# Five places in the engines' instruction lists of a two-layer encoder kernel

## The chip, the cores and the metric

The kernel runs on one core of a Trainium2 chip. A core has a matrix engine (TensorE, PE in the profile; its weight loads are PEld), a vector engine (VectorE, DVE), a scalar engine (ScalarE, ACT), a general engine (GpSimd, POOL) and an engine that here issues transfers (SyncE, SP). Each works through its own list of instructions in order and waits at an instruction until what it needs is there. The metric is the device time of one execution in microseconds; the median of the runs counts.

## The reference

The input is 1024 tokens of width 1024. Layer 0 projects the normed tokens once, and feeds a diagonal state-space part with a gated linear unit (GLU) and a retention part; both are gated, joined and projected back. Layer 1 is a convolution of width 31. Cut to what the change lies in:

```python
def s5_mixer(...):                       # y of the state-space scan
    y = jax.nn.gelu(y)
    y = y * jax.nn.sigmoid(y @ glu_w + glu_b)

def retention(q, k, v):                  # 8 heads, chunks of 64 tokens
    q = rope(q, positions) * (RET_DK ** -0.5)
    k = rope(k, positions)
    ...

def mixer_ab(h, ...):
    u_s5, g_s5, q, k, v, g_ret = jnp.split(h @ w_in, cuts, axis=-1)
    y_s5 = s5_mixer(u_s5, ...) * jax.nn.silu(g_s5)
    y_ret = retention(q, k, v) * jax.nn.silu(g_ret)
    return jnp.concatenate([y_s5, y_ret], axis=-1) @ w_out

def mixer_conv(h, ...):
    a, b, g = jnp.split(h @ w_in, 3, axis=-1)
    u = depthwise_conv(a * jax.nn.sigmoid(b), conv_w) + conv_b
    u = jax.nn.silu(layernorm(u)) * jax.nn.silu(g)
    return u @ w_out
```

Each layer is x + mixer(rmsnorm(x)), and a last rmsnorm ends it. All is float32.

## The kernel before

Everything lies in tiles of 128 partitions; a product works on 128 x 512 halves of the tokens. For accuracy each operand of a matmul is split into a high part in the matmul's reduced type (made by a copy on ACT, names ending in h, wh_...) and a low part, the remainder (names ending in l, wl_...), and `mm3` (lines 217 to 226) makes each product of three: high by high (line 224), high weight by low operand (225) and low weight by high operand (226). Weights come in as wf_..., ACT makes wh_... (line 213), and POOL or DVE makes wl_... (line 214).

The program is written out in one long order by a tile framework. `tc.issue_after(i)` puts what is issued within it behind instruction i in the list of its engine; a scheduler decides the rest by priorities. Tiles with the same tag share a few buffers, so that a new one waits for the last use of an old one: the tag "tp" has three (`load_split`, 1346). At the end `order` (lines 287 to 301) adds a set of pairs (engine, late, early): in that engine's list the n-th instruction that writes the tile `late` has to stand behind the n-th that writes `early`. Such a pair adds no wait between engines; it sets the order within one list, and the scheduler places everything else around it.

The stages that matter, in the order of time:

- `retention` (1070) goes through four pairs of heads. For each it makes keys and queries (`ret_proj`, 1121: kraw, qraw on DVE at 1138; turned by a rotary product on POOL at 1151 and 1153, krot, qrot and the swapped halves kswp, qswp), values (`ret_values`, 1171, three matmuls at 1185 to 1187 and an ACT copy at 1188; for the first pair `ret_values_wide`, 1193, matmuls 1209 to 1211, with the low weights wl_v0_0_j) and the heads (`ret_heads`).
- Between them lies work of the state-space part. `y_pass(k)` (1020) loads y (yp, line 1027), takes its GELU on ACT (1031, yn), stores it (1033), makes four differences of its quarters on DVE (1039 to 1042), splits these and stores the parts (1048, 1049, t_d). `glu_sums(g)` (1051) loads quarters of the GLU's weights (gs0, gs1, line 1058), combines them on DVE (1062 to 1065) and stores the sums (1068, ws_d). These serve a product in seven block multiplications instead of eight.
- `layer0_back_and_layer1` (1336) makes the GLU. `load_split` (1346) loads an operand (line 1356), and `split` (1331) makes its high part on ACT (1332) and its low part on DVE (1334), with an optional `behind`. `product` (1386) puts four k-blocks of `mm3` into a bank. The last of the block multiplications, at 1459 to 1474, makes mm_glu5n of yt1, adds u3 into a spare bank on DVE (mm_gluz, line 1470), goes on in the same bank with y22 and adds u2 (1473). `gated` (1396) loads the gate yg and yn (1398, 1400), takes a tanh on ACT (1409), multiplies on POOL (1401) and DVE (1414) and splits the result (ysh 1416, ysl 1418).
- Then line 1475 loads the retention's results as operands (yr0 for the first half of the tokens, yr1 for the second, eight tiles each), and `w_out` multiplies both by the output weights (mm_wo, with the weights wos and wor).
- Layer 1: `h1` (1500) makes the normed operands (h1h 1513, h1l 1514), `ab` the products and u (1542), `conv` (1566) the convolution, a chain of taps on DVE (1607), for which ACT and POOL make partial sums (tp at 1575, 1579, 1580, copied to a bank at 1586). Its norm takes sums over partitions by matmuls of ones (cst, 557) and a square root and reciprocal (523, 524).

Of the kernel before, what the change touches and what calls it, by code (L numbers as in the profile page):

```python
# [15 lines left out]
ALU = mybir.AluOpType  # L16
# [6 lines left out]
KB = 8  # L23
# [13 lines left out]


LANES = 2


def s5_order():

    seq = []
    for b in range(8):
        g, h = 8 + 2 * b, 9 + 2 * b
        turns = [(f"m0_{b}", 0), (f"m1_{b}", 0)]
        kern = [(f"Kg_{b}", 0), (f"Kg_{b}", 1)]
        z = [(f"v{c}_{b}", n) for n in range(4) for c in range(2)]
        back = [(f"d0_{b}", 0), (f"d1_{b}", 0), *z[6:], (f"S_{b}", 0), (f"S_{b}", 1)]  # L50
        w = [(f"{t}_{b + 1}", n) for t, n in (("W2r", 0), ("W2i", 0), ("pw0", 0), ("pw1", 0), ("W2r", 1), ("W2i", 1))]
        w = w if b < 7 else []
        seq += [*kern, *turns, *z[:6]]
        if b:
            seq += [*back, (f"gt_{g}", 0), (f"wl_g{h}", 0), *w[:3], (f"gt_{g}", 1), *w[3:]]
        else:
            seq += [(f"gt_{g}", 0), *w, *back, (f"gt_{g}", 1)]
        seq += [(f"gt_{h}", 0), *([(f"wl_g{g + 2}", 0)] if b < 7 else []), (f"gt_{h}", 1)]
    return [("PE", ("mm_g8_0", 6), ("v1_0", 7)),
            *(("Activation", (f"pw0_{b + 1}", 0), (f"gt_{8 + 2 * b}", 0)) for b in range(1, 7)),  # L60
            *(("DVE", late, early) for early, late in zip(seq, seq[1:]))]
# [4 lines left out]
def mv(ap):  # L66

    return ap.rearrange("p (a c) -> p c a", a=LANES)


def un(ap):

    return ap.rearrange("p (c a) -> p a c", a=LANES)


def nat(ap):

    return ap.rearrange("p (a c) -> p a c", a=LANES)

# [15 lines left out]
class Trunk:  # L95
# [148 lines left out]
    def run(self):  # L244
        tc, nc, A = self.tc, self.nc, self.A
        self.ps_mm = self.pool("ps_mm", 3, PSUM)
        self.cp = self.pool("cp")
        self.wp = self.pool("wp")
        self.opA = self.pool("opA", 16)
        self.dram = self.pool("dram", 1, DRAM)  # L250

        self.ident = self.cp.tile([P, P], F32, name="ident")
        make_identity(nc, self.ident)
        self.ones = self.cp.tile([P, P], F32, name="ones")
        nc.vector.memset(self.ones[:], 1.0)
        self.ones_r = self.cp.tile([P, P], F32R, name="ones_r")
        nc.vector.tensor_copy(self.ones_r[:], self.ones[:])
        self.epst = self.cp.tile([P, 1], F32, name="epst")
        nc.vector.memset(self.epst[:], EPS)
        self.mhalf = self.cp.tile([P, KB], F32, name="mhalf")  # L260
        nc.vector.memset(self.mhalf[:], -0.5)
        self.warm = self.cp.tile([P, 1], F32, name="warm")
        nc.scalar.copy(self.warm[:], self.ones[:, 0:1])

        dt = lambda n, shape: self.dram.tile(shape, F32, name=n)
        self.u_d = dt("u_d", [8, 8, 16, 8, P])
        self.y_d = dt("y_d", [8, 8, 16, 8, P])
        self.k_d = dt("k_d", [8, 112 + P, P])
        self.gs_d = dt("gs_d", [D, T])
        self.gr_d = dt("gr_d", [D, T])  # L270
        self.yn_d = dt("yn_d", [D, T])
        self.yr_d = dt("yr_d", [D, T])
        self.t_d = dt("t_d", [2, 2, HALF, T])
        self.x1_d = dt("x1_d", [D, T])

        with ExitStack() as mid:
            self.mid = self.pool("mid", 1, stack=mid)
            with ExitStack() as st:
                self.layer0_front(st)
            with ExitStack() as st:  # L280
                self.ps_aux = self.pool("ps_aux", 5, PSUM, stack=st)
                self.retention(st)
        with ExitStack() as st:
            self.layer0_back_and_layer1(st)
        self.order(s5_order())

    def order(self, pairs):

# [15 lines left out]
    def layer0_front(self, st):  # L304
# [107 lines left out]
        def u_block(nb):  # L412
            ut = uv.tile([P, 8, P], F32, name=f"ut_{nb}", tag="ut", bufs=2)

            def evac(h, ps):
                r = self.R[:, h * HALF:(h + 1) * HALF]
                o = ut[:, ::-1, h * 64:(h + 1) * 64].rearrange("p j (a m) -> p j a m", a=LANES)

                with self.tc.issue_after(self.u_evac[0].ins) if nb == 1 else nullcontext():
                    self.u_evac[nb] = nc.vector.tensor_tensor(  # L420
                        o, ps[:].rearrange("p (m j a) -> p j a m", j=8, a=LANES),
                        r.rearrange("p (a m j) -> p j a m", j=8, a=LANES), op=ALU.mult)
            if nb < 3:
# [912 lines left out]
    def layer0_back_and_layer1(self, st):  # L1336
        nc, A = self.nc, self.A
        v, gp = nc.vector, nc.gpsimd
# [4 lines left out]
        hs = lambda h: slice(h * HALF, (h + 1) * HALF)  # L1343
        rows = lambda k: slice(k * P, (k + 1) * P)

        def load_split(parts, name, h, wide, behind=None):

            res = []
            for i, part in enumerate(parts):
                if wide:  # L1350
                    if i % 2 == 0:
                        f2 = self.wp.tile([P, 2, HALF], F32, name=f"{name}f{i}", tag="wf", bufs=3)
                    f = f2[:, i % 2, :]
                else:
                    f = lp.tile([P, HALF], F32, name=f"{name}f{i}", tag="tp", bufs=3)[:]
                nc.sync.dma_start(f, part)
                a, b = (self.op_tile(self.opA, f"A{h}", f"{name}{q}{i}") for q in "hl")
                self.split(f, a, b, v, behind)
                res.append((a, b))
            return res  # L1360
# [21 lines left out]
        u3 = [opB.tile([P, HALF], F32, name=f"gu3_{n}", tag="B1") for n in range(4)]  # L1382
# [3 lines left out]
        def product(ps, w, a, x, more=False):  # L1386

            for k in range(4):
                self.mm3(ps[:], w, 4 * a + k, (x[k][0][:], x[k][1][:]), k == 0 and not more, k == 3, more)

        def spare(name, n):
            return ps_cv.tile([P, HALF], F32, name=name, tag=("cv", "cn")[n % 2])

        held = []

        def gated(nb, h, z, turned=False):
            yg = lp.tile([P, HALF], F32, name=f"yg{nb}_{h}", tag="u", bufs=5)
# [27 lines left out]
        for m in range(2):  # L1425
            pss = [self.bank(f"mm_glu1{2 * m + a}", aux=False) for a in range(2)]
# [13 lines left out]
        for i, x in ((6, t2), (7, t3), (4, t4)):  # L1440
            for m in range(2):
# [5 lines left out]
                for a in range(2):  # L1447
                    n = 2 * m + a
                    ps = self.bank(f"mm_glu{i}{n}", aux=False)
                    product(ps, w, a, x)  # L1450
                    if i == 4:
                        z = spare(f"mm_gluy{n}", n)
# [8 lines left out]
        for m in range(2):  # L1461
            pss = [self.bank(f"mm_glu5{2 * m + a}", aux=False) for a in range(2)]
            for i, x in ((5, t1), (3, b22)):
                w = wn()
                for a in range(2):
                    n = 2 * m + a
                    product(pss[a], w, a, x, i == 3)
                    if i == 5:
                        z = spare(f"mm_gluz{n}", n)
                        v.tensor_tensor(nat(z[:]), un(u3[n][:]), un(pss[a][:]), op=ALU.add)  # L1470
                        gated(4 + n, 1, z, True)
                    else:
                        v.tensor_tensor(pss[a][:], u2[n][:], pss[a][:], op=ALU.add)
                        glu_end = gated(n, 1, pss[a])
        yr = [load_split([self.yr_d[rows(k), hs(h)] for k in range(KB)], f"yr{h}", h, False) for h in range(2)]


        hx = [None, None]
# [521 lines left out]
```

## Time and profile before

| | |
|---|---|
| median of three runs | 1142.86 us (1140.91, 1142.86, 1143.72) |
| profiled execution, its own time | 1140.13 us |
| its span, first to last instruction | 1138.3 us |
| mean granted TensorE clock | 0.997 |
| busy: PE, DVE, ACT, POOL | 1119.0, 832.9, 492.3, 640.0 us |
| HBM read and written | 182.53 MB, 74.65 MB |

A row of a group or of the timeline names the line of the code, the engine, the operation and the tiles as out<-in (numbers of the tiles left out), with its start and duration in microseconds; what is in square brackets at its end is the idle time of the engine just before it and what ended that. The rows of waits give who waited, for whom, and how long in total, how often and at most. A window gives each engine's busy time in a stretch. A matmul's duration overlaps the next one's, so what TensorE loses is read from the starts.

### The profile page before, as it was taken

What the parts mean: (1) busy time and instruction counts of PE and PEld (TensorE: products, weight loads), DVE (VectorE), ACT (ScalarE), POOL (GpSimd) and SP (SyncE); (2) the same over time, 40 slices, a digit from 0 to 9 for tenths busy, and PEclk for the clock granted to TensorE, in tenths of its full rate; (3) what the DMA queues carried; (4) which work ended last, traced back from release to release, by engine and by line L of the source; (5) the groups of instructions that cost most, each with busy time, mean ns of one, the idle gap of its engine ahead of it and who ended that gap; (6) DMA issues with size and microseconds to landing.
All of it is one profiled execution on the core that took longest, in us unless ns stands there. A gap on an engine that the chain in (4) does not pass through costs nothing.

```text
span 1138.3 us, 17193 instructions
## 1 busy us (share of the span) xinstructions
PE 1119.0 (98%) x6278; PEld 979.4 (86%) x6278; DVE 832.9 (73%) x1478; ACT 492.3 (43%) x723; POOL 640.0 (56%) x448
## 2 busy tenths in 40 slices
PE   9999999999999999999999999999999999999897
PEld 7888888888888889898888888888888888888786
DVE  7973967777417469587669523599999899999744
ACT  6422433333223231333546324455536676444673
POOL 2059999888136454332674110688534568677663
PEclk9999999999999999999999999999999999999999
DMA  9345555553487866869998987666678655367865
GB/s 356 111 132 158 195 181 180 170 176 133 150 263 251 302 221 176 314 194 348 390 354 290 339 298 268 222 218 211 221 269 293 222 188 173 111 205 243 285 225 189
DMA packets 118181, 262.51 MB, mean 231 GB/s; under 512 B 10704, under 2 KB 42320, under 8 KB 117456
## 3 DMA queue, kind: packets, MB, share of 16 engines
q1 hardware_dynamic: 114640, 248.82, 64.8%
q10 hardware_dynamic: 3456, 12.58, 2.7%
q8 instruction: 49, 0.80, 0.3%
q14 instruction: 36, 0.29, 0.1%
HBM read 182.53 MB, written 74.65 MB: 226 GB/s over the span
## 4 chain that ended last, share of the span: by engine, by line
PE 74%; DMA 10%; DVE 8%; ACT 3%; issue 2%; POOL 1%; SPq 1%; POOLq 0%; DVEq 0%; ACTq 0%
PE mm_g L224 6%; PE mm_g L225 6%; PE mm_g L226 6%; PE mm_wo L225 5%; PE mm_wo L224 5%; PE mm_wo L226 5%; DMA yp<-y_d 2%; PE mm_b L225 2%; PE mm_b L226 2%; PE mm_a L226 2%; PE mm_a L225 2%; PE mm_b L224 2%; PE mm_a L224 2%; PE mm_oc L226 2%; PE mm_oc L225 2%
## 5 line engine op out<-in xcount | busy, mean ns | idle before, releaser
L1607 DVE SCALAR_TENSOR_TENSOR cv<-u,convw,cv 128x512 f32<-128x512 f32 x398 | 273.0, 748 | 6.5 <-ACT cv L1586 4.5
L1580 POOL TENSOR_TENSOR tp<-tp,tp 128x512 f32<-128x512 f32 x64 | 83.1, 1298 | 33.8 <-ACT tp L1579 32.8
L224 PE MATMUL mm_g<-xh,wh_g 128*128 128x512 f32 x256 | 97.9, 382 | 0.0
L225 PE MATMUL mm_g<-xl,wh_g 128*128 128x512 f32 x256 | 97.0, 379 | 0.0
L226 PE MATMUL mm_g<-xh,wl_g 128*128 128x512 f32 x256 | 95.7, 379 | 0.0
L485 POOL TENSOR_TENSOR s1q<-s1q,s1q 128x512 f32<-128x512 f32 x12 | 17.6, 1470 | 79.4 <-ACT s1q L480 79.4
L1579 ACT ACTIVATE tp<-u,convw 128x512 f32<-128x512 f32 x64 | 45.4, 718 | 34.5 <-POOL tp L1580 33.8
L224 PEld LDWEIGHTS mm_g<-xh,wh_g 128*128 128x128 f32 x256 | 48.8, 191 | 6.8 <-issue 0.2
L435 DVE TENSOR_TENSOR gt<-mm_g,R 128x512 f32<-128x512 f32 x32 | 21.9, 687 | 44.5 <-PE mm_g L226 44.4
L226 PEld LDWEIGHTS mm_g<-xh,wl_g 128*128 128x128 f32 x256 | 48.4, 189 | 6.9
L225 PEld LDWEIGHTS mm_g<-xl,wh_g 128*128 128x128 f32 x256 | 48.4, 189 | 6.6
L226 PE MATMUL mm_oc<-zh,wl_woc 128*128 128x512 f32 (+1 forms) x144 | 51.0, 357 | 0.3 <-DMA wl_woc<-lo_woc 0.3
L214 POOL TENSOR_TENSOR wl_glu<-wf_glu,wh_glu 128x1024 fp32r<-128x1024 f32 x14 | 33.9, 2423 | 30.9 <-ACT wh_glu L213 30.9
L225 PE MATMUL mm_oc<-zl,wh_woc 128*128 128x512 f32 (+1 forms) x144 | 51.1, 356 | 0.0
L224 PE MATMUL mm_oc<-zh,wh_woc 128*128 128x512 f32 (+1 forms) x144 | 51.0, 366 | 0.0
L224 PE MATMUL mm_g<-h1h,wh_cg 128*128 128x512 f32 x128 | 48.9, 382 | 0.0
L224 PE MATMUL mm_wo<-ysh,wh_wos 128*128 128x512 f32 x128 | 48.9, 382 | 0.0
L225 PE MATMUL mm_b<-h1l,wh_cb 128*128 128x512 f32 x128 | 48.7, 381 | 0.2
L225 PE MATMUL mm_u<-xl,wh_u 128*128 128x512 f32 x128 | 48.1, 380 | 0.7 <-DVE xl L358 0.7
L226 PE MATMUL mm_b<-h1h,wl_cb 128*128 128x512 f32 x128 | 48.6, 380 | 0.0
L225 PE MATMUL mm_wo<-ysl,wh_wos 128*128 128x512 f32 x128 | 48.5, 379 | 0.0
L226 PE MATMUL mm_wo<-ysh,wl_wos 128*128 128x512 f32 x128 | 48.5, 379 | 0.0
(528 smaller groups left out, 3590.0 us busy)
## 6 DMA issues: line engine op xcount, KB each, us to landing
wf_g<-w_ab SPq DMA_DIRECT2D x16, 512.0 KB, 6.0
wf_wos<-w_out SPq DMA_DIRECT2D x16, 512.0 KB, 4.2
wf_wor<-w_out SPq DMA_DIRECT2D x16, 512.0 KB, 5.3
wf_cb<-w_c SPq DMA_DIRECT2D x16, 512.0 KB, 4.1
wf_ca<-w_c SPq DMA_DIRECT2D x16, 512.0 KB, 5.2
wf_woc<-w_out_c SPq DMA_DIRECT2D x16, 512.0 KB, 7.2
wf_v<-w_v SPq DMA_DIRECT2D x12, 512.0 KB
wf_cg<-w_c SPq DMA_DIRECT2D x11, 512.0 KB, 4.2
```

The lines of the kernel that those rows point to most:

```text
L214: self.low_made = lo[i].tensor_tensor(wl[:].rearrange(fl)[:, c], wf[:, c], h.bitcast(F32), op=ALU.subtract)
L224: nc.tensor.matmul(ps, wh[:, kb, :], xh, start=start, stop=False, **more)
L225: nc.tensor.matmul(ps, wh[:, kb, :], xl, start=False, stop=False, **more)
L226: self.last_mm = nc.tensor.matmul(ps, wl[:, kb, :], xh, start=False, stop=stop, **more)
L435: nc.vector.tensor_tensor(nat(gt[:, c]), un(ps[:]), nat(self.R[:, c]), op=ALU.mult)
L485: nc.gpsimd.tensor_tensor(a, a, sq[:], op=ALU.add)
L1579: nc.scalar.mul(sk[:], u[:, k:k + HALF], cw[:, nb, k:k + 1])
L1580: gp.tensor_tensor(s0[:], s0[:], sk[:], op=ALU.add)
L1607: v.scalar_tensor_tensor(dst[:], *tap, accs_[i][:], op0=ALU.mult, op1=ALU.add)
```

## The change

Four pairs are added to the list that `order` gets, and one `behind`.

- DVE: the first half of kraw_3 (line 1138) stands behind the difference of line 1040 (on yn_2) and no longer between lines 1039 and 1040; line 1041 comes right after it.
- SP: the load of gs1_3 (line 1058) stands behind the last store of the split differences of the pair before (line 1049). With it the stores and loads around it change places: the sums of gs1_3 on DVE come after one piece of the retention's normed results, two stores of these come before the store of the weights' sums, and a later load of yp before the second of these stores.
- DVE: one tap of the convolution (the 24th that writes the bank cv6_0) stands behind the first low part h1l0_1 of layer 1's second half. Thirty microseconds on, this lets the scheduler put other instructions of the norm elsewhere: on ACT the weights' copy and the sigmoid of line 1529 come ahead of a table load and the square root of line 523, and so the copy of line 1586 comes earlier; some taps and products of the second half change places.
- POOL: the product qswp_0 (line 1153) stands behind the low weights wl_v0_0_1.
- The eight low parts of yr0 (line 1334 on DVE) are issued behind the third addition at line 1470 (mm_gluz2). Before, three of them stood ahead of the first such addition and the fourth right behind it. On ACT two of the high parts move behind the casts of the GLU's weights and the gates; on SP the loads yr0f3 to yr0f7 (line 1356) move behind the loads of all gates, the last two of them also behind a further load of output weights, and the loads of yr1 move with them; on POOL a product yg comes ahead of the last low weights of the GLU; TensorE's products of the output weights are interleaved a little differently at their begin.

No instruction is added or taken away.

```diff
--- before.py
+++ after.py
@@ -37,6 +37,12 @@
 LANES = 2
+ORDER = (
+    ('DVE', ('kraw_3', 0), ('yn_2', 0)),
+    ('SP', ('gs1_3', 0), ('t_d', 7)),
+    ('DVE', ('cv6_0', 23), ('h1l0_1', 0)),
+    ('Pool', ('qswp_0', 0), ('wl_v0_0_1', 0)),
+)
@@ -282,7 +288,7 @@
             self.layer0_back_and_layer1(st)
-        self.order(s5_order())
+        self.order(s5_order() + list(ORDER))
@@ -1391,7 +1397,7 @@
-        held = []
+        held, zs_ = [], {}
@@ -1467,12 +1473,12 @@
                     if i == 5:
                         z = spare(f"mm_gluz{n}", n)
-                        v.tensor_tensor(nat(z[:]), un(u3[n][:]), un(pss[a][:]), op=ALU.add)
+                        zs_[n] = v.tensor_tensor(nat(z[:]), un(u3[n][:]), un(pss[a][:]), op=ALU.add)
                         gated(4 + n, 1, z, True)
...
-        yr = [load_split([self.yr_d[rows(k), hs(h)] for k in range(KB)], f"yr{h}", h, False) for h in range(2)]
+        yr = [load_split([self.yr_d[rows(k), hs(h)] for k in range(KB)], f"yr{h}", h, False, zs_[2] if h == 0 else None) for h in range(2)]
```

## The prediction

> **What bounds the kernel now.** I read the summary first, then the chain that ended last, then TensorE's waits by their size, and at last the windows in which the waits fall.
>
> ```profile
> span 1138.3 us, 17193 instructions
> PE 1119.0 (98%) x6278; PEld 979.4 (86%) x6278; DVE 832.9 (73%) x1478; ACT 492.3 (43%) x723; POOL 640.0 (56%) x448
> PE 74%; DMA 10%; DVE 8%; ACT 3%; issue 2%; POOL 1%; SPq 1%; POOLq 0%; DVEq 0%; ACTq 0%
> ```
>
> TensorE is busy for 1119.0 of 1138.3 us and holds 74% of the chain, so the matmuls themselves, which the change does not touch, are nearly the whole time. What an order of instructions can win or lose lies in the 19.3 us between, and in stages where another engine sets the end. The waits say where the 19.3 us are:
>
> ```profile
> PE cst L557 <- DVE cs L1689: 3.2, 1, 3.2
> PE mm_glu L224 <- DVE mm_gluz L1470: 2.3, 1, 2.3
> PE mm_v L1185 <- ACT v L1188: 1.3, 2, 1.0
> PE mm_v L1210 <- POOL wl_v L214: 0.7, 1, 0.7
> PE mm_glu L224 <- ACT v L1188: 0.4, 1, 0.4
> ```
>
> The columns are total, times, longest. Four of the five edits stand beside one of these rows: the gate product of line 1470, the values' copies of line 1188 (twice), the values' low weights of line 214. The first row, the convolution's sums, is the end of layer 1's DVE work.
>
> ```profile
> 580.00:600.00 20.00, 17.70 (x81) 14.67 (x79) 13.59 (x20) 11.32 (x18) 15.30 (x9) 1.00 0.97 333
> 720.00:740.00 20.00, 20.00 (x94) 17.53 (x93) 9.22 (x13) 9.83 (x13) 13.15 (x7) 1.00 0.66 232
> 740.00:760.00 20.00, 20.00 (x94) 17.50 (x94) 19.93 (x31) 10.61 (x16) 16.56 (x11) 1.00 0.61 210
> 900.00:920.00 20.00, 20.00 (x102) 17.73 (x101) 13.05 (x25) 14.26 (x22) 11.87 (x10) 1.00 0.71 264
> 1060.00:1080.00 20.00, 16.78 (x66) 12.72 (x65) 14.95 (x24) 14.43 (x21) 11.12 (x8) 0.91 0.78 256
> ```
>
> After window and length come busy time and count of PE, PEld, DVE, ACT, POOL, then the granted clock, the DMA share and GB/s. A full window holds 94 wide matmuls, 0.213 us each (20/94). Around 590 there are 81: 13 x 0.213 = 2.8 us lost. From 740 on DVE is full (19.93 of 20), so that layer 1 goes at DVE's pace until TensorE waits 3.2 us at its end. This matters for every gain made earlier: it counts only if DVE starts layer 1 earlier too. The window before, 720 to 740, says that it would: DVE works 9.22 of 20 us and TensorE all 20, so there DVE waits for TensorE.
>
> **The change part by part.**
>
> *The load of w_glu behind the store t_d (SP).* SP's list loses its place for one issue, and that is all that the store and the next load, yp, gain.
>
> ```profile
> 456.04 0.64 SPq L1058 DMA_DIRECT2D gs<-w_glu  x1
> 457.47 0.42 SPq L1027 DMA_DIRECT2D yp<-y_d  x1
> ...
> 464.06 1.28 ACT L1031 ACT_TABLE_LOAD   x1 [4.84 <-DMA yp<-y_d]
> 467.24 1.19 ACT L1188 ACTIVATE v<-mm_v,Rtok 128x256 f32<-128x256 f32 x3
> ...
> 467.76 0.38 PE L1185 MATMUL mm_v<-wh_v,xh 128*128 128x256 f32 x1 [1.00 <-ACT v L1188]
> ```
>
> ACT holds the GELU of the loaded tile ahead of the copies of line 1188; yp landed at 464.06, the copies began at 467.24 and TensorE had waited 1.00 by 467.76. The gap of 0.40 between the issue's end (456.68) and the store behind it closes in part: I replay the three issues back to back and get yp out at 457.2, 0.27 earlier. The two ends are 0 (the landing is set by the transfers of that stretch) and 1.00, the whole wait. I take 0.3, the replayed shift, since the replay moves one issue and no work. The gs1 load lands about half a microsecond later, and the additions on it stand behind other DVE work. Below nothing this can hardly go for more than that half microsecond.
>
> *kraw behind the first subtraction of the GELU output (DVE).* Two neighbours change places, so nothing is added:
>
> ```profile
> 481.43 0.68 DVE L1138 TENSOR_TENSOR kraw<-mm_k,R 128x512 f32<-128x512 f32 x1
> 482.75 1.64 DVE L1041 TENSOR_TENSOR yn<-yn,yn 128x512 f32<-128x512 f32 x1
> ...
> 482.40 1.44 POOL L1151 TENSOR_TENSOR krot<-kraw,ropek 128x512 f32<-128x512 f32 x1 [7.14 <-PE sp L1265]
> ...
> 520.58 0.38 PE L1185 MATMUL mm_v<-wh_v,xh 128*128 128x256 f32 x1 [0.33 <-ACT v L1188]
> ...
> 527.53 0.48 PE L224 MATMUL mm_glu<-y11h,wh_glu 128*128 128x512 f32 x1 [0.44 <-ACT v L1188]
> ```
>
> krot starts on POOL when kraw is done. Line 1041 starts 0.35 us after it and takes 1.64 instead of the 0.68 of its neighbour: it ends 0.55 after krot's end at 483.84. With kraw a place later krot starts some 0.6 later, behind the start of line 1041, which then takes 0.68: 0.96 us off the chain of subtractions, their stores and the loads that come back from them. Behind that chain stand the waits of 0.33 and 0.44, both on copies that ACT does after a GELU. Since the first shortens the distance to the second, they can shrink by 0.77 together at most; the other end is 0 (the store's and load's landings hide it) or, if krot were late, a loss of 0.6, for which I see nobody within 40 us who waits for it. I take 0.7, near the upper end, as 0.96 covers both.
>
> On this row the skill has a mechanism: the Trainium skill, page "SBUF — State Buffer", section "Who interferes with whom", says that a vector instruction with two SBUF inputs and a GpSimd instruction that reads SBUF exclude one another for the whole instruction, and that the first to start wins. The 1.64 agrees, and by this rule krot would now be the one to wait; but the same rule speaks against the next edit, since a moved low part that meets a 2.37 us POOL instruction is held again. If one such hold of 1.7 us (2.37 - 0.68) stood before a gate to which my replay leaves 1.2 us, the sum would be 2.7 in place of 3.2.
>
> *The first residual's low parts behind the third gate (DVE, with ACT, SP, POOL behind them).*
>
> ```profile
> 596.86 1.37 DVE L1334 TENSOR_TENSOR yr0l<-yr0f,yr0h 128x512 fp32r<-128x512 f32 x1
> 599.35 0.68 DVE L1470 TENSOR_TENSOR mm_gluz<-gu,mm_glu 128x512 f32<-128x512 f32 x1
> 599.95 2.29 DVE L1334 TENSOR_TENSOR yr0l<-yr0f,yr0h 128x512 fp32r<-128x512 f32 x1
> ...
> 594.67 1.13 ACT L1332 CAST yr0h<-yr0f 128x512 fp32r<-128x512 f32 x2
> 597.13 0.67 ACT L1409 ACTIVATE mm_gluy<-mm_gluy,hgb 128x512 f32<-128x512 f32 x1
> ...
> 599.32 2.37 POOL L214 TENSOR_TENSOR wl_glu<-wf_glu,wh_glu 128x1024 fp32r<-128x1024 f32 x1
> 605.67 1.29 POOL L1401 TENSOR_TENSOR yg<-yg,yn 128x512 f32<-128x512 f32 x1
> ...
> 600.09 0.48 PE L224 MATMUL mm_glu<-y22h,wh_glu 128*128 128x512 f32 x1 [2.32 <-DVE mm_gluz L1470]
> ```
>
> TensorE starts at 600.09 what the gate product of 599.35 (ended 600.03) set free. Before that product the old list has three of the low parts, 0.6 + 0.6 + 1.3 of DVE's time by their starts; without them it could begin 2.5 earlier. But its neighbour, the product with the gate, waits for ACT's tanh of 597.13, which moves up by the two casts' time only in part (the weight's cast stands there too): I get 596.3 for the tanh, 597.0 to 597.7 for the product behind it, 597.6 to 598.28 for line 1470, and TensorE on again at 598.35, 1.74 earlier. Then what is late next: twelve matmuls later, at 598.35 + 2.56 = 600.91, TensorE wants the low weights that POOL makes from 599.32 to 601.69. The two products before them would run at 1.29 each, the undisturbed row, and give POOL back 0.4, so they are there at 601.3. TensorE waits 0.4 there, and 1.4 of the 1.74 is left. Ends: 2.32, the wait itself, and 0.96 if POOL gains nothing; worse only through the transfers, next.
>
> The low parts are no fewer, so 8 x 0.68 come later on DVE, and the first of them keep their buffers longer. The pool "tp" has three, so the load yr0f3 waits for the first low part, and SP's queue gets five loads at later places, behind all the gates' loads, the sixth and seventh behind the weight load that stands at about 616.7:
>
> ```profile
> 617.17 3.36 SPq L1356 DMA_DIRECT2D yr1f<-yr_d  x3
> ...
> DMA to landing us min/median/max: 4.0/4.9/5.9
> ...
> L1356 SPq DMA_DIRECT2D y21f<-yn_d x4: 319/834/977, 518.6 to 525.1; - x4
> L1332 ACT CAST y21h<-y21f x4: 617/619/622, 526.5 to 530.6; 128x512 fp32r<-128x512 f32 x4
> ...
> 620.48 0.38 PE L224 MATMUL mm_wo<-yr0h,wh_wor 128*128 128x512 f32 x1
> ```
>
> Where yr1f stands now, at 617.2, yr0f6 will stand. With the 4.9 us of the yr0f rows and 0.62 for the cast it is ready at 622.7. TensorE wants it six k-blocks of 0.64 behind 620.48, so at 624.3, less the gain of 1.4: 622.9. That is covered, by 0.2 us. With 5.9 us it would be 0.8 late. I take no loss, as the median covers it, and keep this for the third rival.
>
> *The convolution's tap behind the first low part of layer 1 (DVE).*
>
> ```profile
> 881.54 3.09 DVE L1514 SCALAR_TENSOR_TENSOR h1l<-x1n,vecs,h1h 128x512 fp32r<-128x512 f32 x3
> ...
> 907.57 3.13 DVE L1607 SCALAR_TENSOR_TENSOR cv<-u,convw,cv 128x512 f32<-128x512 f32 x4 [3.04 <-ACT cv L1586]
> 913.31 0.18 DVE L524 RECIPROCAL cn<-cn 128x4 f32<-128x4 f32 x1 [1.02 <-ACT cn L523]
> 916.64 1.41 DVE L1607 SCALAR_TENSOR_TENSOR cv<-u,convw,cv 128x512 f32<-128x512 f32 x2 [1.04 <-ACT cv L1586]
> ```
>
> The first h1l comes one tap, 0.7 us, earlier, but the three take 3.09, so one of them is held, and TensorE's need there is met by the later ones; nothing is won at 881. The tap moves ACT's list thirty microseconds on: in the changed program the copy of line 1586 (before at 916) stands before the table load of line 523. So DVE's wait at 916.64 goes, 1.04, while the reciprocal waits about 0.9 longer, during which DVE has a tap more to do. Of the two waits, 2.06, I expect 1.3 to stay: a gain of 0.8. As DVE sets the end from here to 1066, it reaches the end. Ends: 2.06, and -1.3 if the table load holds the reciprocal with no tap left to fill the time.
>
> *The rotary product behind the values' low weights (POOL).* In the changed program POOL's list has the two where they were: that edit orders what already was in this order, and a program without it has the same five lists. Nothing is gained, and the wait of 0.7 on line 214, which belongs to a later piece of the weights, stays.
>
> **Sum:** 0.3 + 0.7 + 1.4 + 0.8 + 0 = 3.2 us. The profiled execution took 1140.13, its span of 1138.3 and 1.8 around it; that is 2.7 below the median of the runs, 1142.86. So 1136.9 for such an execution, and 1142.86 - 3.2 = 1139.7 for the median.
>
> **The rivals.** *Larger:* POOL's low weights are early enough after all and the gate's wait goes whole (2.32), and the waits around 913 close (2.06). With 0.3 and 0.7 that makes 5.4: 1137.5. For it speaks that POOL's products near 597 run beside DVE's low parts, which go; against it, POOL's list, which has that weight behind them. With each term at its upper end (1.00 + 0.77 + 2.32 + 2.06 = 6.15) it would be 1136.7.
>
> *Swallowed:* layer 1 ends when DVE is done with the taps, whatever happens before 700, and the table load eats the rest. Then 0 to 0.8 is left, about 1142.4. The full DVE windows speak for it, the 9.22 of 720 to 740 against.
>
> *Slower:* the loads yr0f6 and yr0f7 land late. It decides from a landing of about 5.1 us on (622.9 - 617.2 - 0.62). The transfers in this kernel do take longer at times: y21f was issued at 518.6 and cast at 526.5, 7.9 us. With that, and 0.9 for the wait for one of three buffers, the cast is done at 626.6, TensorE stands 3.7 us; the low part adds 0.7, and the loads of the second half, yr1f, which queue behind, cost some 2.3 more. 6.7 - 3.2 = 3.5 us slower, 1146.4. Against it: eight yr0f loads took 4.0 to 5.9, in a stretch whose DMA share was 0.97 around 590.
>
> **How the numbers follow.** A measurement of this kernel cannot tell less than about 0.3%, 3.4 us, from no change. Forecast 0.42 (its terms' ends give 1138.3 to 1141.7 for it alone; about half, 0.23, lies beyond 3.4 us), larger 0.27, swallowed 0.12, slower 0.19 (0.17 beyond 3.4 us). Faster 0.23 + 0.27 = 0.50, slower 0.17, same the remaining 0.33. The range begins at 1135.3, the upper ends' 1136.7 less the 1.4 by which runs lie off their median (1140.91 to 1143.72 is 2.8 wide), and goes to 1146.0, just short of the slower rival's price.
>
> **What would show it.** The gate's row among TensorE's waits falls from 2.3 to nothing and a row "mm_glu <- POOL wl_glu" of about 0.4 comes in; line 1041 near 482 takes 0.7; the 1.0 and 0.4 on line 1188 shrink; "mm_v <- POOL wl_v" stays at 0.7; DVE's idle between 912 and 917 falls from 2.06 to about 1.3. Wrong would be: a new wait of mm_wo on yr0h or yr0l, or on the transfers behind them (slower rival); the wait at the convolution's sums growing by what the earlier ones lost (swallowed).

## The result, and the profile after

The changed kernel took 1137.14 us in the median of 8 runs (1133.51 to 1140.01), the kernel before 1143.11 in 8 runs beside them. The ratio is 0.9949 with an interval of 0.9929 to 0.9970: 5.8 us faster, between 3.4 and 8.1. The forecast was 1139.7, 3.2 us faster; the time lies in the range, nearest to the rival "larger".

The profiled execution took 1134.49 us. Its summary and TensorE's waits (line numbers of the changed program are 6 higher than before; each kernel below has its own):

```profile
span 1132.7 us, 17192 instructions
PE 1116.6 (99%) x6278; PEld 979.7 (86%) x6278; DVE 829.8 (73%) x1478; ACT 492.5 (43%) x723; POOL 638.3 (56%) x448
```

```profile
PE cst L563 <- DVE cs L1695: 2.9, 1, 2.9
PE mm_glu L230 <- ACT v L1194: 1.2, 1, 1.2
...
PE mm_v L1191 <- ACT v L1194: 1.1, 1, 1.1
...
PE mm_glu L230 <- DVE mm_gluz L1476: 0.5, 1, 0.5
PE mm_glu L230 <- ACT sg L1415: 0.5, 1, 0.5
```

The gate's row fell from 2.3 to 0.5, and no row of POOL's wl_glu came in its place. But the rows on line 1194 (1188 before) did not shrink as forecast: the wait of 1.00 near 467 is 1.05, and while the 0.33 near 520 is gone, the 0.44 near 527 became 1.25. The 0.7 for POOL's wl_v, which should have stayed, is gone, though nothing around it was changed. The two waits as the timeline has them:

```profile
526.96 0.48 PE L230 MATMUL mm_glu<-y11h,wh_glu 128*128 128x512 f32 x1 [1.25 <-ACT v L1194]
...
597.66 0.48 PE L230 MATMUL mm_glu<-y22h,wh_glu 128*128 128x512 f32 x1 [0.53 <-DVE mm_gluz L1476]
```

The windows of the same stages (columns as in the prediction's fence):

```profile
578.00:598.00 20.00, 19.48 (x91) 16.74 (x90) 12.34 (x17) 10.65 (x16) 15.51 (x10) 1.00 0.92 332
718.00:738.00 20.00, 20.00 (x94) 17.53 (x93) 9.45 (x13) 9.82 (x13) 13.28 (x8) 1.00 0.68 236
...
898.00:918.00 20.00, 20.00 (x102) 17.71 (x101) 14.06 (x27) 13.01 (x22) 11.26 (x9) 1.00 0.73 264
1058.00:1078.00 20.00, 17.06 (x76) 13.88 (x75) 16.11 (x26) 16.02 (x24) 12.35 (x9) 1.00 0.79 250
```

Around 590 TensorE does 91 matmuls in place of 81. DVE still waits for TensorE before layer 1 (9.45 of 20). And one thing differs that no step of the prediction had: in the last window the clock is 1.00 where it was 0.91, with 76 matmuls in place of 66.

Where the 5.6 us between the two spans went is read from the starts of four matmuls that both programs have: the one behind the wait near 467, the second product behind the sums near 868, the first of the convolution's sums, and the second product behind the final norm's first sums. Before:

```profile
868.98 0.38 PE L225 MATMUL mm_g<-h1l,wh_cg 128*128 128x512 f32 x1
...
1066.16 2.03 PE L557 MATMUL cst<-cs,ones 128*128 128x512 f32 x2 [3.22 <-DVE cs L1689]
...
1101.11 0.38 PE L225 MATMUL mm_oc<-zl,wh_woc 128*128 128x512 f32 x1
```

After:

```profile
866.46 0.38 PE L231 MATMUL mm_g<-h1l,wh_cg 128*128 128x512 f32 x1
...
1062.78 0.70 PE L563 MATMUL cst<-cs,ones 128*128 128x512 f32 x1 [2.94 <-DVE cs L1695]
...
1095.46 0.38 PE L231 MATMUL mm_oc<-zl,wh_woc 128*128 128x512 f32 x1
```

The differences of these starts, in the same way for every profile of this study (ratio and medians are of the timed runs):

| kernel | to 467 | 467 to 868 | 868 to sums | behind the sums | ratio (interval) | median, before beside it |
|---|---|---|---|---|---|---|
| before | 467.8 | 401.2 | 197.2 | 35.0 | | |
| the change | 467.1 | 399.3 | 196.3 | 32.7 | 0.9949 (0.9929 to 0.9970) | 1137.14, 1143.11 |
| e1 gate | 466.0 | 400.2 | 199.4 | 33.4 | 0.9980 (0.9960 to 1.0000) | 1139.41, 1142.71 |
| e2 tap | 467.4 | 401.7 | 196.4 | 34.4 | 0.9975 (0.9960 to 0.9990) | 1139.82, 1142.71 |
| e3 kraw | 467.9 | 402.5 | 199.0 | 34.8 | 0.9988 (0.9974 to 1.0003) | 1142.04, 1142.71 |
| e4 SP | 467.2 | 405.0 | 198.6 | 35.5 | 1.0001 (0.9985 to 1.0016) | 1142.92, 1142.71 |
| e5 gate's store first | 467.4 | 402.1 | 196.7 | 34.9 | 0.9996 (0.9976 to 1.0015) | 1140.54, 1142.36 |
| e6 table behind | 466.9 | 401.5 | 197.4 | 33.4 | 1.0010 (0.9990 to 1.0031) | 1143.23, 1142.36 |
| e7 change, y21 behind | 467.3 | 401.0 | 196.4 | 32.7 | 0.9945 (0.9926 to 0.9964) | 1136.52, 1142.36 |
| e8 change, gate later | 468.4 | 399.8 | 196.3 | 34.4 | 0.9952 (0.9936 to 0.9968) | 1137.62, 1142.36 |
| e9 gate and tap | 466.7 | 399.8 | 196.3 | 35.6 | 0.9969 (0.9954 to 0.9984) | 1137.58, 1141.57 |
| e10 change again | 466.4 | 400.4 | 196.3 | 32.7 | 0.9960 (0.9941 to 0.9979) | 1135.84, 1141.57 |
| e11 e5 and e6 | 467.8 | 402.0 | 197.5 | 35.0 | 1.0005 (0.9989 to 1.0022) | 1141.25, 1141.57 |
| e12 POOL | 469.3 | 401.2 | 198.7 | 34.7 | 1.0007 (0.9992 to 1.0023) | 1142.82, 1141.57 |

The first column scatters over 3.3 us in programs that hardly differ there, the last over 3 us. The third is the sharpest: six profiles with the tap's pair lie between 196.30 and 196.43. e4's 405.0 stands apart: its profile has a wait of 2.48 near 522 and, as shown at the end, a low clock behind the gate.

### The profile page after: what moved, and what is told of

It is laid out like the page before. It is cut to its first block, busy times and chain, and to the rows that moved or that the text cites. A ratio compares the mean times of both kernels' runs of the same rounds, so it can differ in the third digit from the quotient of the medians.

```text
span 1132.7 us, 17192 instructions
## 1 busy us (share of the span) xinstructions
PE 1116.6 (99%) x6278; PEld 979.7 (86%) x6278; DVE 829.8 (73%) x1478; ACT 492.5 (43%) x723; POOL 638.3 (56%) x448
## 4 chain that ended last, share of the span: by engine, by line
PE 35%; DVE 16%; DMA 4%; issue 1%; POOL 1%; ACT 1%; POOLq 0%; SPq 0%; DVEq 0%; ACTq 0%
DVE cv L1613 12%; PE mm_wo L230 5%; PE mm_wo L231 5%; PE mm_wo L232 5%; PE mm_oc L230 2%; PE mm_oc L232 2%; PE mm_oc L231 2%; PE mm_b L232 1%; PE mm_a L232 1%; PE mm_a L231 1%; PE mm_b L231 1%; PE mm_b L230 1%; PE mm_a L230 1%; DMA yn<-yn_d 1%; PE mm_glu L230 1%
## 5 line engine op out<-in xcount | busy, mean ns | idle before, releaser
L232 PE MATMUL mm_g<-h1h,wl_cg 128*128 128x512 f32 x128 | 48.5, 379 | 0.0
```

The costliest lines, as they stand in the source:

```text
L232: self.last_mm = nc.tensor.matmul(ps, wl[:, kb, :], xh, start=False, stop=stop, **more)
```

## The experiments

**e1, the gate's part alone, and e2, the tap's pair alone.** Theory: the gain is a sum of places, about 2 us at 600 and 1 to 1.4 in the convolution. Rival: it is the clock behind the sums.

```diff
-        self.order(s5_order() + list(ORDER))
+        self.order(s5_order())              # e1: load_split(..., zs_[2] if h == 0 else None) kept
+        self.order(s5_order() + [('DVE', ('cv6_0', 23), ('h1l0_1', 0))])   # e2: zs_ left out
```

> Only the low parts of yr0 behind the third gate addition; the four ordered pairs left out. Theory 'sum of places': the wait of TensorE on line 1470's addition near 600 falls from 2.3 to about 0.5, nothing new is waited for up to 700 and layer 1 begins earlier by it, so 1.8 to 2.2 us faster than before (ratio about 0.998). Rival 'the clock': the gain of the whole change is the clock behind the wait at the convolution's sums and the scatter of transfers, and what is won at 600 is lost again by 870: within 0.5 us of before, with TensorE at line 514's operands (866 to 868) no earlier against the addition at 600 than before.

> Only the pair of the tap and the first low part of layer 1. Theory 'sum of places': DVE's wait of 1.04 for the copy of line 1586 near 916 is gone, that for the reciprocal stays at 1.0, and the time from the first low part of layer 1's second half (882) to the sums (1066) is 1.0 to 1.4 shorter: 1 to 1.4 us faster (ratio about 0.999). Rival 'the clock': that stretch is as long as before within 0.3, and the time moves by the clock in the 5 us behind the sums alone, which can be low or full in either program.

Measured: 0.9980 and 0.9975, 2.3 and 2.9 us, where e1's interval just reaches 1.0000. Their sum, 5.2, is near the 5.8 of the whole change. In e1 the gate's wait is 0.6, but a new one stands behind it, of the kind that the third rival named:

```profile
621.92 0.48 PE L226 MATMUL mm_wo<-yr0h,wh_wor 128*128 128x512 f32 x1 [0.71 <-ACT yr0h L1334]
```

It costs 0.7 and no more; in the whole change's two profiles it is not there. Over all, the stretch from 467 to 868 takes 401.9 in the median of the eight profiles without the gate's part and 400.0 in the six with it. So the gate keeps 1.85 us up to layer 1. With the tap's pair the stretch of the convolution is not 1.0 to 1.4 but, against e1, 3.0 shorter. DVE's waits in that stretch show why, in before, e1 and e2:

```profile
DVE cv L1607 <- ACT cv L1586: 4.1, 2, 3.0
DVE u L1542 <- PE mm_a L226: 1.6, 1, 1.6
DVE cn L524 <- ACT cn L523: 1.0, 1, 1.0
```

```profile
DVE cv L1609 <- ACT cv L1588: 6.5, 3, 3.0
DVE u L1544 <- PE mm_a L228: 1.6, 1, 1.6
DVE cn L526 <- ACT cn L525: 1.0, 1, 1.0
```

```profile
DVE cv L1610 <- ACT cv L1589: 3.5, 1, 3.5
DVE u L1545 <- PE mm_a L229: 1.2, 1, 1.2
DVE cn L527 <- ACT cn L526: 1.0, 1, 1.0
```

There is a third wait for the copy of line 1586, 2.41 near 995 in e1, which the one profile shown of before happens not to have: its wait was 0. With the tap's pair the second (916) and the third are gone. The wait for TensorE's mm_a is 0.4 shorter, but the next one, for ACT's copy near 907, is 0.4 longer (3.5 in place of 3.0), so that nothing is kept of it.

**e3, kraw's pair alone, and e4, SP's alone.**

```diff
+        self.order(s5_order() + [('DVE', ('kraw_3', 0), ('yn_2', 0))])    # e3
+        self.order(s5_order() + [('SP', ('gs1_3', 0), ('t_d', 7))])       # e4
```

> Only the pair of kraw and the difference of line 1040. Theory 'the cast in front': line 1041 near 482 takes 0.7 in place of 1.6, the copy of line 1188 near 520 is on time, so its 0.33 is gone, but the wait near 527 grows by the same, because ACT's list holds the copies behind the cast of y21h, whose load lands no earlier: TensorE starts mm_glu on y11 within 0.3 of before and the time is within 0.3 us of before. Rival, as predicted: both waits shrink, 0.7 us faster.

> Only the pair of the load of gs1_3 and the store t_d. Theory: the load of yp goes out 0.1 to 0.3 earlier but the table load on ACT, which waits for its landing, moves by less than 0.1 against the values' matmuls, so the wait of 1.0 near 467 stays between 0.9 and 1.1: nothing, within 0.3 us. Rival, as predicted: that wait falls to 0.7, 0.3 us faster; upper end 1.0.

Measured: 0.9988 with an interval over 1, and 1.0001. Neither can be told from nothing in the time. In e3's profile both waits on line 1188 were longer (0.91 near 521, 1.62 near 529), against both theories; the stretch to 868 is 402.5, no better than before. The cause of the wait near 527 is seen in the changed kernel's ACT:

```profile
525.91 0.62 ACT L1338 CAST y21h<-y21f 128x512 fp32r<-128x512 f32 x1 [6.61 <-DMA y21f<-yn_d]
526.44 0.83 ACT L1194 ACTIVATE v<-mm_v,Rtok 128x256 f32<-128x256 f32 x2
```

ACT stands 6.61 us at the cast of y21h for its load; the values' copies, whose input is ready, are behind it, and TensorE behind them. Counted from the matmul near 467, the changed kernel issued that load 0.73 earlier than before (50.10 against 50.83) and had it no earlier (58.79 against 58.72). What the chain of differences won, the transfer kept. The other profiles show no gain either: from the wait near 467 to the start of mm_glu near 527 the four with kraw's pair and this wait took 59.7 to 61.4 us, eight without the pair 59.8 to 60.7. SP's pair shows only in the wait near 467: 0.78 to 1.16 in the five profiles with it (median 0.90), 1.00 to 1.94 in the nine without (median 1.08).

**e5 and e6, two exchanges on ACT in the kernel before.** Theory: the third wait comes from the place of one store. The gate's SiLU (sgg3_0, line 1554; the expectations call it a sigmoid) stands behind a partial sum that waits for its buffer; its store, the load of it (gl, line 1738), POOL's product of it and then the sums behind that product all follow.

```diff
+        self.order(s5_order() + [('Activation', ('tp6_1_0', 0), ('sgg3_0', 0))])   # e5
+        self.order(s5_order() + [('Activation', ('cn4_3_0', 0), ('sb2_1', 0))])    # e6
```

> The kernel before with one pair of neighbours on ACT exchanged: the sigmoid of layer 1's gate (sgg3_0, line 1554) ahead of the partial sum tp6_1_0 (line 1575), which waits for DVE. The tapped programs have them in this order. Theory 'third wait': the store of the gate goes out 1.7 us earlier after the addition of line 514's stage (868), the load gl and POOL's product behind it too, and DVE's third wait for the copy of line 1586, near 995 (0, 2.4, 2.4 and 1.6 us in the four profiles without the tap's pair), falls to 0 to 0.7; the waits at 907, 913 and 916 stay; 1 to 2 us faster than before. Rival 'landings': the wait near 995 comes from how long the store takes to land (2.0 to 4.3) and not from its place; it stays between 0 and 2.4, and the time within 0.5 us of before.

> The kernel before with the square root of line 523 (and its table load) behind the sigmoid of line 1529 on ACT, and nothing of the tap: the part of the tap's knock-on near 913. Theory: DVE's wait of 1.04 near 916 is gone and the third wait near 995 is still there in its scatter (0 to 2.4), since the gate's store keeps its place; the stretch from 868 to 1066 takes 196.2 to 198.5; 0.5 to 1.2 us faster. Rival 'all of the tap's gain is here': as the tap alone, no wait near 995 and 196.3 for the stretch; 2.5 us or more faster.

SP's list in e1, and then in e5:

```profile
972.95 0.33 SPq L1557 DMA_DIRECT2D gs_d<-sgg  x1
977.14 0.33 SPq L1740 DMA_DIRECT2D gl<-gs_d  x1
```

```profile
974.48 0.33 SPq L1555 DMA_DIRECT2D gs_d<-sgg  x1
978.06 0.33 SPq L1738 DMA_DIRECT2D gl<-gs_d  x1
```

Counted from the second product behind the sums (866.22 in e1, 869.46 in e5) the store goes out at 106.7 in e1 and at 105.0 in e5. In both it took long until the load could follow (4.2 and 3.6, against 2.3 in the profile of before), yet e5 has no third wait, and the stretch is 196.7. So the place decides whether a slow landing is felt. All 14 profiles fit this: the third wait goes by when POOL's product of the loaded gate can start, in us behind the same matmul. Where that is 109.8 to 112.1 there is no third wait (the six with the tap's pair, e5, e11 and before), at 112.4 it is 0.45 (e6), and at 113.4 to 114.3 it is 1.6 to 2.4 (e1, e3, e4, e12). An earlier store keeps the start on the right side of this even when its landing is slow. The rival "landings" falls, in the profile. In the time nothing is seen: 0.9996, with an interval that holds the 1.5 us expected as well as nothing.

e6 took the wait near 916 away and kept a third one of 0.45, as expected; but the reciprocal waits 1.7 in place of 1.0, and the time is not the 0.5 to 1.2 us better that the theory had (1.0010).

**e11, both exchanges together.**

```diff
+        self.order(s5_order() + [('Activation', ('tp6_1_0', 0), ('sgg3_0', 0)), ('Activation', ('cn4_3_0', 0), ('sb2_1', 0))])
```

> The kernel before with both exchanges on ACT (the gate's sigmoid ahead of the partial sum, the square root behind the sigmoid of line 1529), the tap left where it was. Theory 'the knock-on is the gain': no wait near 916, none near 995, 868 to 1066 in 196.3 to 197.0, and the time 1.5 to 2.9 us faster than before, as with the tap's pair. Rival 'the order of DVE's taps': the stretch stays above 197.3.

```profile
DVE cv L1607 <- ACT cv L1586: 3.0, 1, 3.0
DVE cn L524 <- ACT cn L523: 1.6, 1, 1.6
DVE u L1542 <- PE mm_a L226: 1.6, 1, 1.6
DVE x L1769 <- DMA x1l<-x_d: 0.5, 1, 0.5
```

The waits near 916 and 995 are gone, but the stretch is 197.5, 1.2 longer than with the tap's pair and 1.2 shorter than the median of the five profiles with neither (198.7). This is the sign that the rival named (above 197.3), but the profiles point to another reason than the order of the taps. Of the 1.2, 0.5 is a wait for the load x1l near the end, which comes and goes in the profiles without the tap's pair (0 to 0.5) and is 0 in the six with it. The reciprocal's wait, 1.65 and not 1.02, makes 0.6, and that lies on ACT too: with the tap's pair the weights' cast of line 190 is made where ACT otherwise waits 0.5 for POOL's partial sum, and the table load and the square root behind it come 0.8 earlier.

How much of the tap's gain is which wait is read better from e5, which takes away the third wait alone: 196.7, that is 2.0 of the 2.4 between 198.7 and 196.3. Without their third wait and their wait for x1l the five old profiles would lie at 196.7 to 196.8. So the third wait is most of it, and 0.4 is left for the waits near 907 to 916; the 1.04 near 916 is not kept whole, because with it gone an addition of line 1769 (0.6 us) now stands on DVE ahead of cs, the input of the first sums.

The times do not bear this out: the tap's pair alone gave 2.9 us (1.1 to 4.6), e5 and e11 nothing that can be seen, and e11's interval allows 1.3 us at most. The theory that the knock-on on ACT is the gain is thus not shown. What else of the tap's pair counts in the time stays open.

**e7, the whole change with the cast of y21h out of the way, and e8, with the low parts later still.**

```diff
+    ('Activation', ('y21h0', 0), ('v_3', 7)),      # e7, added to ORDER
-    ..., zs_[2] if h == 0 else None)               # e8
+    ..., zs_[3] if h == 0 else None)
```

> The whole change, and on ACT the first cast of y21h behind the last copy of the values (v_3) in place of ahead of three of them. Theory 'the cast in front': TensorE's wait near 527 (1.25 after the change, 0.44 before) falls to 0 to 0.3, the y21 operands are ready about 1.5 later and still in time, and TensorE keeps 1 us: 0.8 to 1.2 us faster than the change, ratio to before about 0.994. Rival 'transfers': TensorE only waits some us later for y21 or the block behind it, or at 551; the same as the change.

> The whole change with the low parts of yr0 behind the fourth addition of line 1470 in place of the third, some 5 us later still, with the loads behind them. Theory: the loads yr0f have little slack left (0.2 by the prediction; the gate's part alone showed a wait of 0.7 for yr0h near 622), so TensorE waits 2 to 6 us more for yr0h or yr0l in mm_wo: 2 to 6 us slower than the change. Rival: loads are early enough, within 0.5 us of the change.

e7: the wait near 527 is gone, and TensorE stands 25 us later instead:

```profile
552.59 0.48 PE L230 MATMUL mm_glu<-y11h,wh_glu 128*128 128x512 f32 x1 [2.29 <-ACT sg L1415]
```

It was 0.48 there with the change. The rival held: 0.9945 against 0.9949, the same. ACT's list leads back to a load again:

```profile
541.05 1.04 ACT L219 CAST wh_glu<-wf_glu 128x1024 fp32r<-128x1024 f32 x1 [9.12 <-DMA wf_glu<-w_glu]
```

The tanh that TensorE waits for starts 10.8 us behind this cast in e7 and in the change alike, and the cast starts, counted from 467, 0.9 later in e7 (73.8 against 72.9). In these profiles the loads set the pace, and a wait taken away comes back at the next place.

e8: no loss, 0.9952, and no wait for yr0h or yr0l, though the one yr0f load whose landing its profile gives took 5.9 us. The scheduler moves TensorE's products with yr0 back too: 12 of them stand in a row ahead of the next products with ysh, where the change has 18 or 19. The theory of little slack falls.

**e9, gate and tap without the other three; e10, the whole again; e12, POOL's pair alone.**

```diff
 ORDER = (
-    ('DVE', ('kraw_3', 0), ('yn_2', 0)),
-    ('SP', ('gs1_3', 0), ('t_d', 7)),
     ('DVE', ('cv6_0', 23), ('h1l0_1', 0)),
-    ('Pool', ('qswp_0', 0), ('wl_v0_0_1', 0)),
 )
```

> The low parts of yr0 behind the gate and the tap's pair, without the pairs of kraw, of SP and of POOL. Theory 'two of five places': the whole gain is here: as fast as the whole change run beside it, within 1 us, ratio to before 0.995 to 0.997. Rival 'retention counts too': kraw's pair gave 1.4 us in its own run, and without it the kernel is 1 to 2 us slower than the whole change, ratio 0.9965 or more.

> The whole change once more, for more runs and a second profile. Theory: ratio 0.994 to 0.997; in the profile the gate's wait 0.5 to 0.9, 868 to 1066 in 196.3 (after its own zero), the wait near 527 between 0.9 and 1.6 on the copies of line 1188, and the part before 456, which the change does not touch, anywhere within 1.5 us of the other profiles. Rival 'the clock': the stretch behind the sums is again as short as in the first profile (32.7 against 35.0 before).

> Only POOL's pair, which leaves all five lists as before. Theory: the same program, ratio 1.000, its interval about 0.0015 to each side, which shows what a comparison tells from nothing; TensorE's wait for POOL's wl_v near 354, 0.7 before, is anywhere from 0 to 1.4, as in the other profiles. Rival: 0.3 us or more faster, with that wait gone.

e9 gave 0.9969 and e10 0.9960 beside it: medians 1137.58 and 1135.84. The 1.7 between them is what the rival "retention counts too" had, and more than the 1 us that the theory allowed; but the intervals overlap, and the profiles show no such gain up to the second product near 868 (866.5 in both e9 and the change, 866.7 in e10). Gate and tap hold at least the larger part, and whether kraw's and SP's pairs add a microsecond to them these runs do not tell. e10 repeats the first profile: 0.4 at the gate, 196.3 in the convolution, and the 32.7 behind the sums that its rival "the clock" had. e12 shows what nothing looks like: the same lists, ratio 1.0007, and in its profile a wait for POOL's wl_v of 1.2 at a place where before had 0.7 and the change none.

## Why the prediction was right, and where not

- *The gate* was right in mechanism: the product of line 1470 waited behind low parts, and without them TensorE's wait is 1.8 us shorter (2.32 to 0.53; forecast 1.74). It is 0.4 to 0.7 in all six profiles with this part and 1.6 to 2.4 in the eight without. The wait for POOL's low weights, put at 0.4, did not come in the changed kernel (0.2 in e7). In its place some of the gain goes to the loads (0.7 at 622 in e1 and e9). Net 1.85 against 1.4. Two of the moved low parts were indeed held (1.77 and 1.59 us in place of 0.68), as the working feared, but no wait of TensorE came of it.
- *The tap* is the term that was mis-sized: 0.8 forecast; 0.9 against the one profile that the sum was made on, but 2.4 against the median of five profiles with the old order. The nearness of 0.9 is partly luck, as 0.4 of it is that profile's wait for x1l, which the forecast did not count. The forecast had right that the wait near 916 goes, and that nothing is won at 881. It missed the third wait near 995, as the profile at hand had none. And it read ACT's new list wrongly. ACT before, and then after:

```profile
911.68 1.28 ACT L523 ACT_TABLE_LOAD   x1
...
914.23 1.28 ACT L1529 ACT_TABLE_LOAD   x1
915.52 0.60 ACT L1529 ACTIVATE sb<-mm_b 128x512 f32<-128x512 f32 x1
916.02 0.59 ACT L1586 COPY cv<-tp 128x512 f32<-128x512 f32 x1
```

```profile
909.18 0.59 ACT L1535 ACTIVATE sb<-mm_b 128x512 f32<-128x512 f32 x1
909.79 1.28 ACT L529 ACT_TABLE_LOAD   x1
911.08 0.30 ACT L529 ACTIVATE cn<-cn,epst 128x4 f32<-128x4 f32 x1
911.29 0.58 ACT L1592 COPY cv<-tp 128x512 f32<-128x512 f32 x1
```

  The copy does not stand before the table load but behind the square root. It comes 2.2 earlier against the second product near 868, because the activation sb goes ahead and the second table load no longer stands between. The reciprocal therefore did not wait 0.9 longer (1.02 and 1.02); e6 and e11 show that it does wait longer when the tap stays (1.7 and 1.6).
- *kraw's pair*: line 1041 went from 1.64 to 0.68, as forecast. The 0.7 behind it failed: the bound named for its lower end, that the landings hide it, is what happened. The transfers set when y21 is there.

```profile
482.12 0.68 DVE L1047 TENSOR_TENSOR yn<-yn,yn 128x512 f32<-128x512 f32 x1
...
482.34 1.59 POOL L1157 TENSOR_TENSOR krot<-kraw,ropek 128x512 f32<-128x512 f32 x1 [7.72 <-DVE kraw L1144]
```

  Now krot starts second, during line 1041, and takes 1.59, where the undisturbed krot near 497 took 1.27 before. That agrees with the rule of the Trainium skill, "SBUF — State Buffer", section "Who interferes with whom", that of two such instructions the later one is blocked. So does the old order: there krot started during line 1040, which also has two inputs in SBUF, and took 1.44, and then blocked line 1041. The exchange thus made krot 0.15 longer.
- *SP's pair*: 0.3 forecast, 0.2 in the medians of the wait, whose ranges overlap, and nothing that the time can show. *POOL's pair*: nothing, as forecast.
- *The rivals.* "Swallowed" is out: what was won at 600 is there at 868 in six profiles. "Slower" is out as a whole, though its mechanism is seen with 0.7. "Larger" came nearest in time, partly by another way than it said: the gate's wait went almost whole, but of the 2.06 near 913 only 1.04. In the price of "slower", the 0.9 for a buffer and the 2.3 for yr1f stand on no row, and no run shows them.
- *What the sum had not*: the stretch behind the sums, and the clock there, below. At a clock of 1.00 that stretch takes 32.7 in three profiles with the tap's pair and 33.4 in e1's, the one without it that has full clock and no further wait. The medians of the other stretches give 1.85 + 2.35 + 0.2 = 4.4 us, inside both intervals of the whole change (3.4 to 8.1, and 2.4 to 6.7 in e10). With the 0.7 behind the sums they are 5.1.
- *The range* held, but the terms erred in both directions: kraw's 0.7 did not come, and gate and tap brought 0.45 and 1.55 more than forecast. The narrower 1138.3 to 1141.7, called the ends of the terms, is not what the ends as written add up to.

## What to carry to other kernels

One profile shows one draw of the waits that hang on transfers: where a list has no slack behind a load, price the wait that a slower landing would bring, and not only the waits that are there. An order pair is best read by what it moves far away; here most of what the tap's pair won in the profiles, 2.0 of 2.4, lay in a store a hundred microseconds on. And where loads set the pace, taking a wait away only moves it: ask first what the next place waits for.

## What the runs showed of the hardware

The granted clock behind TensorE's wait at the convolution's sums is not settled by that wait's length. e10 and e9 both waited 2.94 us there; the windows of 12 us from 1058 on, e10 first:

```profile
1058.00:1070.00 12.00, 9.06 (x38) 6.88 (x37) 8.70 (x13) 7.77 (x12) 5.22 (x4) 1.00 0.77 249
```

```profile
1058.00:1070.00 12.00, 9.06 (x25) 5.83 (x24) 6.99 (x11) 6.42 (x10) 4.91 (x3) 0.72 0.75 243
```

At 1.00 the stretch behind the sums takes 32.7 us, at 0.72 it takes 35.6. In windows of 2 us e9's clock is 0.50 from 1062 to 1068. Nine of the 14 profiles have such a drop here, behind waits of 2.7 to 3.6 us, and five have none, behind waits of 2.3 to 3.3. Shorter waits can bring the same: e4's at the gate, 2.15 us long, was followed by this window, with 0.50 in its middle, from 604 to 606.

```profile
602.00:608.00 6.00, 6.00 (x20) 4.98 (x21) 5.72 (x7) 3.96 (x8) 5.95 (x4) 0.72 0.96 326
```

Before's own wait there, 2.32, was not: its clock stayed at 1.00, as it did in the six other profiles without the gate's part (waits of 1.58 to 2.44). The Trainium skill, "TensorE: Matmul & The Clock Gate", in Part 1 has the clock halve after at least one idle window of about 3.4 us, free-running. Here drops stand behind waits of 2.15 and 2.94; the half and the outcome that varies from run to run agree with it, the length does not.

So a wait taken away may win more than itself, namely the chance of such a drop. The mean granted clock of the timed runs fits this: below 0.997 it was in 39 of 98 runs of the kernel before and in 34 of 72 of the six kernels with neither gate nor tap, but in 5 of 36 of e1, e2 and e9 and in 3 of 34 of the change, e7, e8 and e10. At 0.997 alone, e9 took 1138.05 in the mean (9 runs) and before, beside it, 1140.97 (9 runs): 2.9 us, where the means of all their runs differ by 3.8. So the waits themselves would be the larger part of this gain. This is a comparison of runs, not an experiment on the clock; that the removed waits cause it was not tried by itself.
